# Sparse attention: the causal mask added to the scores in PSUM by VectorE, in one instruction with the row maximum

## The chip, the cores and the metric

The kernel runs on one core of a Trainium2 chip. The metric is the device time of one execution in microseconds (us). A core has five engines that take their instructions in a fixed order each, and wait for each other by semaphores: TensorE (PE in the profile; PEld is its weight load), VectorE (DVE), ScalarE (ACT), GpSimd (POOL) and SyncE (SP), which here issues the loads. TensorE writes its products to PSUM, eight banks of 128 partitions x 512 fp32; VectorE and ScalarE read and write both PSUM and SBUF.

## The reference

One decoder layer over 256 tokens of width 2048: gated linear attention and native sparse attention (NSA) beside each other, one output projection, then a SwiGLU FFN. The change lies in two of NSA's three branches, the selected blocks and the sliding window:

```
qh = rms_norm(heads(q, NSA_HEADS), q_g)          # 8 heads in 2 key/value groups
ss = einsum(qb, ks) * scale                      # selected blocks
ps = softmax(where(kpos <= t, ss, NEG))
o_sel = einsum(ps, vs)
sw = einsum(qb, kwb) * scale                     # sliding window
pw = softmax(where((wpos >= 0) & (dist >= 0) & (dist < WINDOW), sw, NEG))
o_win = einsum(pw, vwb)
```

With 256 tokens there are 4 blocks of 64 and all of them are selected (up to 16 may be), and the window of 512 covers the sequence. So both branches are plain causal attention, each with its own keys and values.

## The kernel before

Tokens are worked on in two tiles of 128 (t = 0, 1). The large products (L297 in `chunk`, L1178 in `gate_up`) are done in fp32 halves: a ScalarE copy makes the high part "hi" of a weight (L144), VectorE subtracts it to make the low part "lo" (L145, function `split`), and TensorE sums x_hi w_hi + x_hi w_lo + x_lo w_hi. One row of L145 makes the low part of two blocks of 128 weight rows, which then serve 12 matmuls.

The program is written as generators. `drive` runs a main one (a projection) and, for so many of its matmuls, one step of a side task: `gla_mix`, then `nsa_mix`. A scheduler then fixes each engine's order, so main and side matmuls alternate on TensorE. NSA runs beside the last piece of the query projection and beside `w_out_half(0)`, the first half of the output projection. It has four tiles of work, key/value group kv = 0, 1 by token tile t = 0, 1. For each of them `nsa_scores` works on four heads j, both branches b in one bank (view `sv`, 128 queries x 2 branches x ns keys, ns = 128 or 256):

- three matmuls (L902) make the scores in fp32 halves;
- a fourth product (L904) adds the mask to the last 128 keys of both branches: the stationary matrix is a bf16 identity `identb`, the moving one `cneg`, 0 or -1e30, in bf16 and twice beside each other;
- a short product (L905) makes the scores against the 15 compressed keys, into another bank;
- VectorE takes the maximum of each branch over its ns keys (L908) and scales it (L909);
- ScalarE takes the exponential with that bias and the row sum (L911), out of PSUM.

Then come the softmax of the compressed branch (L914 to L928) and the scaling of the probabilities (L934, eight rows a tile). `nsa_out` transposes the probabilities on TensorE (L215), evicts them in two parts by ScalarE (L665) and VectorE (L666), and multiplies them with the values (L976; L971 for the compressed branch, evicted by L959 and L960). Others that share VectorE in this stretch: L1014, which evicts a finished piece of `w_out_half`, L1110, sums of weight rows for the FFN, and L867 to L874, norms of the second query group.

The constants are made early in `constants()`: GpSimd writes the mask in fp32 to a scratch tile, VectorE casts it and the identity to bf16 (L436, L437).

Of the kernel before, what the change touches and what calls it, by code (L numbers as in the profile page):

```python
# [8 lines left out]
F32 = mybir.dt.float32  # L9
F32R = mybir.dt.float32r  # L10
BF16 = mybir.dt.bfloat16
AF = mybir.ActivationFunctionType
ALU = mybir.AluOpType
AX = mybir.AxisListType

P = 128
# [8 lines left out]
NEG = -1e30  # L25
# [12 lines left out]
def kernel(  # L38
# [4 lines left out]
    nc = tc.nc  # L43
    act, mm = nc.scalar.activation, nc.tensor.matmul
# [8 lines left out]
    cp = tc.alloc_tile_pool(name="cp", bufs=1)  # L53
# [5 lines left out]
    def slot(pool, tag, bufs, align=None):  # L59
        def f(shape, dt=F32):  # L60
            n_tiles[0] += 1
            return pool.tile([P] + list(shape), dt, tag=tag, bufs=bufs, name=f"{tag}_{n_tiles[0]}", align_bytes=align)
        return f
# [3 lines left out]
    g4, g2, g1, small = slot(gp, "g4", 24, LINE), slot(s2p, "g2", 13), slot(s1p, "g1", 7), slot(s1p, "sm", 12)  # L67

    def bank():
        n_tiles[0] += 1  # L70
        return pp.tile([P, 512], F32, tag="bank", name=f"bank_{n_tiles[0]}")
# [136 lines left out]
    ident = kp.tile([P, P], F32, name="ident")  # L208
# [199 lines left out]


    lmask = cp.tile([P, len(MASKED) + 2, P], F32, name="lmask")  # L410
    cneg = cp.tile([P, 2, P], BF16, name="cneg")
    identb = cp.tile([P, P], BF16, name="identb")
    mneg = cp.tile([P, NT, NCMP], F32, name="mneg")
    mone = cp.tile([P, NT, NCMP], F32, name="mone")

    def affine(ap, pattern, base, cm, fill=0.0):
        nc.gpsimd.affine_select(
            out=ap, in_=ap, pattern=pattern, compare_op=ALU.is_ge, fill=fill, base=base, channel_multiplier=cm)

    def constants():  # L420

        nc.gpsimd.memset(lmask, 1.0)
        affine(lmask[:, M_UP, :], [[1, P]], -1, -1)
        affine(lmask[:, M_LOW, :], [[-1, P]], -1, 1)
        for li, l in enumerate(MASKED):

            nb = P // (2 * l)
            v = lmask[:, li, :].rearrange("p (b h i) -> p b h i", h=2, i=l)
            for half, row0 in ((1, 0), (0, l)):
                affine(v[:, :, half, :], [[-2 * l, nb], [0, l]], -row0, 1)  # L430
                affine(v[:, :, half, :], [[2 * l, nb], [0, l]], row0 + l - 1, -1)

        cnegf = g1([2, P])
        nc.gpsimd.memset(cnegf, 0.0)
        affine(cnegf, [[0, 2], [-1, P]], 0, 1, NEG)
        nc.vector.tensor_copy(cneg, cnegf)  # L436
        nc.vector.tensor_copy(identb, ident)  # L437

        nc.gpsimd.memset(mneg, 0.0)
        affine(mneg, [[P, NT], [-16, NCMP]], -31, 1, NEG)  # L440
        nc.gpsimd.memset(mone, 1.0)
        affine(mone, [[P, NT], [-16, NCMP]], -31, 1, 0.0)
# [329 lines left out]
    def thrice(a):  # L772

        return a.unsqueeze(2).to_broadcast([P, a.shape[1], 3, NCMP])

    def groups(a):
        return a[:, :, :3 * G3].rearrange("p h (g n) -> p h g n", n=G3)[:, :, :, :NCMP]
# [110 lines left out]
    def nsa_scores(kv, t, res):  # L888
        ns, tb = (t + 1) * P, slice(t * P, (t + 1) * P)
        scv = sc[kv][:, t, :]  # L890
        qf, qh, ql = (a[:, :, tb] for a in nq[kv])
        kh, kl = (st[name][:, :, kv, :ns] for name in ("kh", "kl"))
        gv = st["gate"][:, t, 12 * kv:12 * kv + 12].rearrange("p (h b) -> p b h", b=3)
        pr = [g4([2, 2, ns]) for _ in range(2)] if t else [g4([4, 2, ns])]
        pr = [pr[j // 2][:, j % 2] if t else pr[0][:, j] for j in range(4)]
        mxs, nb, sums = small([4, 2]), small([4, 2]), small([4, 2])
        pc_ = bank()
        for j in range(4):
            p = bank()
            sv = p[:, :2 * ns].rearrange("p (b s) -> p b s", b=2)  # L900
            for i, (a, b) in enumerate(((qh, kh), (qh, kl), (ql, kh))):
                mm(sv, a[:, j], b, start=(i == 0), stop=False, skip_group_check=True)  # L902
                yield
            mm(sv[:, :, t * P:], identb, cneg, start=False, stop=True, skip_group_check=True)  # L904
            mm(pc_[:, j * NCMP:(j + 1) * NCMP], qf[:, j], kcm[:, kv * NCMP:(kv + 1) * NCMP],  # L905
               start=True, stop=True)
            yield
            nc.vector.tensor_reduce(mxs[:, j, :], sv, AX.X, ALU.max)  # L908
            TS(nb[:, j, :], mxs[:, j, :], scv[:, j:j + 1], -1.0, ALU.mult, ALU.mult)  # L909
            for b in range(2):  # L910
                act(pr[j][:, b, :], sv[:, b, :], AF.Exp, bias=nb[:, j, b:b + 1], scale=scv[:, j:j + 1],  # L911
                    accum_out=sums[:, j, b:b + 1])

        c = small([4, NCMP])  # L914
        TT(c, pc_[:, :4 * NCMP].rearrange("p (h n) -> p h n", h=4), scv.unsqueeze(2).to_broadcast([P, 4, NCMP]), ALU.mult)
        TT(c, c, mneg[:, t, :].unsqueeze(1).to_broadcast([P, 4, NCMP]), ALU.add)
        mx = small([4])
        nc.vector.tensor_reduce(mx, c, AX.X, ALU.max)
        TT(c, c, mx.unsqueeze(2).to_broadcast([P, 4, NCMP]), ALU.subtract)
        act(c, c, AF.Exp)  # L920
        sm = small([4])
        nc.vector.tensor_reduce(sm, c, AX.X, ALU.add)
        nc.vector.reciprocal(sm, sm)
        TT(sm, sm, gv[:, 0, :], ALU.mult)
        TT(c, c, mone[:, t, :].unsqueeze(1).to_broadcast([P, 4, NCMP]), ALU.mult)
        c3 = g2([4, P])
        nc.gpsimd.memset(c3, 0.0)
        TT(groups(c3), thrice(c), sm.unsqueeze(2).unsqueeze(3).to_broadcast([P, 4, 3, NCMP]), ALU.mult)  # L928
        rs = small([4, 2])
        nc.vector.reciprocal(rs, sums)  # L930
        TT(rs, rs, gv[:, 1:3, :].rearrange("p b h -> p h b"), ALU.mult)
        for j in range(4):
            for b in range(2):
                TS(pr[j][:, b, :], pr[j][:, b, :], rs[:, j, b:b + 1], None, ALU.mult)  # L934
        res.update(pr=pr, c=c3)
# [44 lines left out]
    def nsa_mix():  # L980
        tiles = [(kv, t) for kv in range(2) for t in range(NT)]
        res = {u: {} for u in tiles}

        def ready(u):
            while u[0] not in nq or not all(("key", br, t) in done for br in range(2) for t in range(NT)):
                yield

        for i, u in enumerate(tiles):
            yield from ready(u)
            yield from nsa_scores(*u, res[u])  # L990
            if i:
                yield from nsa_out(*tiles[i - 1], res[tiles[i - 1]])
        for _ in range(2):
            yield
        yield from nsa_out(*tiles[-1], res[tiles[-1]])
# [388 lines left out]

    drive([proj(C_LR, ev_go(0), ((0, 256), (256, 272)), first_chunk)], 2)
    constants()
    background += [sum_rows(f, pair) for f in sorted(SUMS) for pair in SUMS[f]]
    rate[0] = 12
# [56 lines left out]
```

## Time and profile before

| what | value |
|---|---|
| median of 3 runs | 1099.42 us (1099.35 to 1099.77) |
| the profiled execution, its own time | 1099.59 us |
| its span, first to last instruction | 1097.4 us |
| instructions in the trace | 14686 |
| first and last start of L902 | 286.0 and 338.6 us |
| data moved | 271.21 MB, mean 247 GB/s |

The profiled execution is 0.17 us above the median, and 2.2 us of it lie outside its span. The page gives each engine's busy share in 40 slices of 27.4 us each, as tenths:

```profile
PE   9999999999999999999999999999999999999998
DVE  6778879987799988997999999999999999999997
ACT  7755557555675587666585866768585867777785
PEclk9999999999999999999999999999999999999999
```

NSA lies in slices 11 to 14 from the left. TensorE is full everywhere, and its granted clock (PEclk) is full too. TensorE's starts are the reliable part of its rows: the ends are modelled and overlap, so the distance from one start to the next tells what a matmul takes on the path.

### The profile page before, as it was taken

The page shows a single profiled execution, that of the slowest core. Times are in us where ns is not written, and L with a number is a line of the kernel's source. Part 1 is how long each engine was busy: PE and PEld are TensorE (multiplying, and loading weights), DVE is VectorE, ACT ScalarE, POOL GpSimd, SP SyncE. Part 2 cuts the span into 40 slices and gives each one's busy share as a digit, 9 for nine tenths or more (in the row PEclk, how much of TensorE's full clock was granted, in tenths as well). Part 3 has the DMA queues.
Part 4 walks back from the last instruction along what each step waited for, and adds up shares of the span by engine and source line. Part 5 has one row for each costly group of instructions (what it writes and reads, how often), then busy time and mean ns, then how long its engine had stood idle before and what let it go on. Part 6 is the DMA issues. An engine that isn't in the chain of part 4 may idle for free.

```text
span 1097.4 us, 14686 instructions
## 1 busy us (share of the span) xinstructions
PE 1092.1 (100%) x5290; PEld 899.2 (82%) x5290; DVE 996.6 (91%) x1291; ACT 745.6 (68%) x1016; POOL 81.1 (7%) x150
## 2 busy tenths in 40 slices
PE   9999999999999999999999999999999999999998
PEld 8888888987777887888888888888888888888887
DVE  6778879987799988997999999999999999999997
ACT  7755557555675587666585866768585867777785
POOL 4100001032101100100000000000000000000000
PEclk9999999999999999999999999999999999999999
DMA  7999978468886956685576657576565768677663
GB/s 280 355 373 351 376 247 297 165 232 288 305 288 255 322 183 231 226 324 176 183 233 217 212 196 253 173 259 209 203 232 204 256 216 294 203 264 236 224 230 115
DMA packets 128884, 271.21 MB, mean 247 GB/s; under 512 B 7126, under 2 KB 9210, under 8 KB 128812
## 3 DMA queue, kind: packets, MB, share of 16 engines
q1 hardware_dynamic: 115532, 223.68, 59.4%
q0 software_dynamic: 12672, 46.14, 11.5%
q8 instruction: 41, 0.67, 0.2%
q10 hardware_dynamic: 608, 0.47, 0.1%
q14 instruction: 31, 0.25, 0.1%
HBM read 247.19 MB, written 23.07 MB: 246 GB/s over the span
## 4 chain that ended last, share of the span: by engine, by line
PE 94%; DVE 2%; issue 1%; ACT 1%; DMA 1%; SPq 0%; POOL 0%; DVEq 0%; POOLq 0%
PE bank L297 46%; PE bank L1178 39%; PE bank L215 3%; PE bank L1319 2%; DMA g<-in_x_dram 1%; PE bank L976 1%; PE bank L902 1%; DVE lo L145 1%; PE bank L607 0%; PE bank L809 0%; ACT hi L144 0%; ACT g L568 0%; PE bank L905 0%; PE bank L904 0%; POOL sm L218 0%
## 5 line engine op out<-in xcount | busy, mean ns | idle before, releaser
L1178 PE MATMUL bank<-ftwo,g 128*128 128x512 f32 x1842 | 430.6, 393 | 0.2 <-ACT ftwo L665 0.2
L1178 PEld LDWEIGHTS bank<-ftwo,g 128*128 128x128 f32 x1842 | 341.2, 188 | 76.8 <-DVE ftwo L666 3.9
L297 PE MATMUL bank<-hi,g 128*128 128x512 f32 (+1 forms) x1088 | 322.1, 376 | 0.4 <-ACT hi L348 0.4
L666 DVE TENSOR_TENSOR ftwo<-fraw,ftwo 128x1536 fp32r<-128x1536 f32 (+1 forms) x130 | 256.5, 1974 | 7.4 <-ACT ftwo L665 6.7
L665 ACT ACTIVATE ftwo<-fraw 128x1536 fp32r<-128x1536 f32 (+1 forms) x130 | 216.0, 1663 | 27.2 <-DMA fraw<-in_w_up_dram 17.1
L297 PE MATMUL bank<-ftwo,g 128*128 128x512 f32 x960 | 220.6, 390 | 0.0
L297 PEld LDWEIGHTS bank<-hi,g 128*128 128x128 f32 x1088 | 191.5, 188 | 30.6 <-issue 1.0
L297 PEld LDWEIGHTS bank<-ftwo,g 128*128 128x128 f32 x960 | 179.6, 188 | 38.3 <-ACT bank L1290 0.3
L297 PE MATMUL bank<-lo,g 128*128 128x512 f32 (+3 forms) x544 | 193.1, 375 | 0.1
L144 ACT ACTIVATE hi<-raw 128x1024 fp32r<-128x1024 f32 (+3 forms) x124 | 130.7, 1058 | 90.4 <-PE bank L297 67.0
L145 DVE TENSOR_TENSOR lo<-raw,hi 128x1024 fp32r<-128x1024 f32 (+3 forms) x124 | 150.0, 1216 | 33.0 <-ACT hi L144 32.5
L665 ACT ACTIVATE ftwo<-g 128x1024 fp32r<-128x1024 f32 x76 | 80.4, 1057 | 74.9 <-DVE g L1209 54.6
L297 PEld LDWEIGHTS bank<-lo,g 128*128 128x128 f32 x544 | 98.2, 189 | 14.5 <-DVE lo L145 0.3
L666 DVE TENSOR_TENSOR ftwo<-g,ftwo 128x1024 fp32r<-128x1024 f32 x76 | 92.6, 1219 | 10.7 <-ACT ftwo L665 10.7
L666 DVE TENSOR_TENSOR ftwo<-fsum,ftwo 128x1024 fp32r<-128x1024 f32 x76 | 92.5, 1218 | 1.0 <-ACT ftwo L665 1.0
L665 ACT ACTIVATE ftwo<-fsum 128x1024 fp32r<-128x1024 f32 x76 | 79.5, 1048 | 5.9 <-DVE fsum L1211 4.6
L1302 ACT COPY g<-bank 128x512 f32<-128x512 f32 x80 | 45.9, 588 | 38.4 <-PE bank L297 36.8
L1209 DVE TENSOR_TENSOR g<-fraw 128x1024 f32<-128x1024 f32 x54 | 65.2, 1217 | 0.0
L1290 ACT COPY bank<-g 128x512 f32<-128x512 f32 x80 | 45.3, 594 | 14.5 <-DVE f L1239 7.9
L1167 POOL DMA_DIRECT2D g<-sums x20 | 10.6, 532 | 501.9 <-DVE ftwo L666 473.3
L665 ACT ACTIVATE g<-bank 128x512 fp32r<-128x512 f32 x46 | 26.9, 597 | 29.6 <-PE bank L215 21.1
L215 PE MATMUL bank<-ident,g 128*128 128x128 f32 (+3 forms) x232 | 43.1, 276 | 0.1
(251 smaller groups left out, 909.5 us busy)
## 6 DMA issues: line engine op xcount, KB each, us to landing
fraw<-in_w_gate_dram SPq DMA_DIRECT2D x86, 512.0 KB, 3.8
fraw<-in_w_down_dram SPq DMA_DIRECT2D x42, 1024.0 KB, 5.0
raw<-in_w_in_dram SPq DMA_DIRECT2D x36, 1024.0 KB, 6.0
fraw<-in_w_up_dram SPq DMA_DIRECT2D x66, 512.0 KB, 4.8
sums<-g POOLq DMA_DIRECT2D x40, 512.0 KB, 6.5
raw<-in_w_out_dram SPq DMA_DIRECT2D x16, 1024.0 KB, 6.7
g<-in_w_gate_dram SPq DMA_DIRECT2D x20, 512.0 KB, 8.2
g<-in_w_up_dram SPq DMA_DIRECT2D x20, 512.0 KB, 9.9
```

The costliest lines, as they stand in the source:

```text
L144: act(h[:, i:i + n], r[:, k + i:k + i + n], AF.Copy)
L145: last["d"] = TT(o[:, i:i + n], r[:, k + i:k + i + n], f32(h[:, i:i + n]), ALU.subtract)
L215: return nc.tensor.transpose(o, i, ident[:n, :n])
L297: last["mm"] = mm(bk[t], a[:, k, t * P:(t + 1) * P], ws[k][m][:, off:off + w], start=(first_ and k == 0 and i == 0), stop=(end and k == 3 ...
L665: act(hi, ps, AF.Copy)
L666: last["d"] = TT(lo, ps, f32(hi), ALU.subtract)
L902: mm(sv, a[:, j], b, start=(i == 0), stop=False, skip_group_check=True)
L1178: mm(banks[q], x, m, start=todo[q] == total[q], stop=todo[q] == 1)
L1209: TT(s1, r[:, 1:3], r[:, 3:4].to_broadcast([P, 2, 512]), ALU.add)
L1290: last["seed", n] = nc.scalar.copy(banks[qs[n][t]], h_sb[n][:, t, :])
L1302: nc.scalar.copy(h_sb[n][:, t, :], bs[t])
L1319: mm(bk, u, m, start=(first and i == 0), stop=(end and i == 2), skip_group_check=onto)
```

## The change

The mask becomes an fp32 tile of 128 x 128 in SBUF, made by GpSimd alone; the bf16 identity and the two casts go. The product of the identity (L904) goes. In its place VectorE runs, for each head and branch, one fused instruction over the 128 keys of the tile's own block: it adds the mask to the scores, writes the sums back to the bank and takes their maximum. For t = 0 the maximum starts from -1e30; for t = 1 it starts from the maximum over the 128 earlier keys, which a reduction over both branches takes first (`past`).

```
-    cneg = cp.tile([P, 2, P], BF16, name="cneg")
-    identb = cp.tile([P, P], BF16, name="identb")
+    cneg = cp.tile([P, P], F32, name="cneg")
...
-        cnegf = g1([2, P])
-        nc.gpsimd.memset(cnegf, 0.0)
-        affine(cnegf, [[0, 2], [-1, P]], 0, 1, NEG)
-        nc.vector.tensor_copy(cneg, cnegf)
-        nc.vector.tensor_copy(identb, ident)
+        nc.gpsimd.memset(cneg, 0.0)
+        affine(cneg, [[-1, P]], 0, 1, NEG)
...
+        past = small([4, 2]) if t else None
         pc_ = bank()
         for j in range(4):
             p = bank()
             sv = p[:, :2 * ns].rearrange("p (b s) -> p b s", b=2)
             for i, (a, b) in enumerate(((qh, kh), (qh, kl), (ql, kh))):
-                mm(sv, a[:, j], b, start=(i == 0), stop=False, skip_group_check=True)
-                yield
-            mm(sv[:, :, t * P:], identb, cneg, start=False, stop=True, skip_group_check=True)
+                mm(sv, a[:, j], b, start=(i == 0), stop=(i == 2))
+                yield
             mm(pc_[:, j * NCMP:(j + 1) * NCMP], qf[:, j], kcm[:, kv * NCMP:(kv + 1) * NCMP],
                start=True, stop=True)
             yield
-            nc.vector.tensor_reduce(mxs[:, j, :], sv, AX.X, ALU.max)
+            if t:
+                nc.vector.tensor_reduce(past[:, j, :], sv[:, :, :P], AX.X, ALU.max)
+            for b in range(2):
+                own = sv[:, b, t * P:]
+                nc.vector.tensor_tensor_reduce(
+                    own, own, cneg, 1.0, past[:, j, b:b + 1] if t else NEG, ALU.add, ALU.max, mxs[:, j, b:b + 1])
             TS(nb[:, j, :], mxs[:, j, :], scv[:, j:j + 1], -1.0, ALU.mult, ALU.mult)
```

Lines shift: L902 of before is L899 in the changed kernel, L905 is L901, L909 is L910, and what follows is one line on; what stands in between `constants()` and `nsa_scores` is four lines back (L666 is L662). The new reduction is L905 there and the fused instruction L908.

The scheduler sets the order anew. TensorE, at the first head of the first tile, before (`bank_3001` holds its scores, `bank_3000` the compressed ones, the others are main work):

```order
L902 MATMUL bank_3001<-g_322_1985,g_496_2842 128x256
L297 MATMUL bank_2775<-lo_2957,g_58_362 128x512
L904 LDWEIGHTS identb
L904 MATMUL bank_3001<-cneg,identb 128x256
L905 MATMUL bank_3000<-kcm,g_494_2840 128x15
L297 MATMUL bank_2775<-hi_2956,g_59_363 128x512
```

and in the changed kernel:

```order
L899 MATMUL bank_2997<-g_321_1981,g_495_2838 128x256
L297 MATMUL bank_2771<-lo_2953,g_58_361 128x512
L901 MATMUL bank_2996<-kcm,g_493_2836 128x15
L297 MATMUL bank_2771<-hi_2952,g_59_362 128x512
L297 MATMUL bank_3033<-hi_3037,g_421_2504 128x512
```

The matmul of the mask is gone with its weight load; the short product follows the scores directly.

VectorE, before, at the third tile (kv = 1, t = 0), from the sixth to the ninth L145 after the first of `w_out_half(0)` (numbers 6 to 9; `bank_3385` and `bank_3411` are the scores of two heads, `sm` are small tiles):

```order
L145 TENSOR_TENSOR lo_3397<-raw_3394,hi_3396 128x2x512
L666 TENSOR_TENSOR g_579_3269<-bank_3270,g_578_3268 128x4x128
L145 TENSOR_TENSOR lo_3401<-raw_3394,hi_3400 128x2x512
L908 TENSOR_REDUCE sm_3347<-bank_3385 128x2
L908 TENSOR_REDUCE sm_3347<-bank_3411 128x2
L909 TENSOR_SCALAR sm_3348<-sm_3347,sc_3031 128x2 x2
L915 TENSOR_TENSOR sm_3426<-bank_3350,sc_3031 128x60
L145 TENSOR_TENSOR lo_3526<-raw_3523,hi_3525 128x2x512
L916 TENSOR_TENSOR sm_3426<-sm_3426,mneg 128x60
L145 TENSOR_TENSOR lo_3530<-raw_3523,hi_3529 128x2x512
```

In the changed kernel the same two heads behind number 7 (each fused instruction is a row ISA with its maximum fetched by a second row ISA of 128x1):

```order
L145 TENSOR_TENSOR lo_3401<-raw_3394,hi_3400 128x2x512
L908 ISA bank_3386,sm_3348<-bank_3386,cneg 128x128
L908 ISA sm_3348 128x1
L908 ISA bank_3412,sm_3348<-bank_3412,cneg 128x128
L908 ISA sm_3348 128x1
L908 ISA bank_3386,sm_3348<-bank_3386,cneg 128x128
L908 ISA sm_3348 128x1
L908 ISA bank_3412,sm_3348<-bank_3412,cneg 128x128
L908 ISA sm_3348 128x1
L910 TENSOR_SCALAR sm_3349<-sm_3348,sc_3026 128x2 x2
```

and, 17 rows on, what stands directly ahead of numbers 8 and 9:

```order
L929 TENSOR_TENSOR g_617_3439<-sm_3427,sm_3434 128x4x3x15
L935 TENSOR_SCALAR g_597_3347<-g_597_3347,sm_3442 128x128 x8
L662 TENSOR_TENSOR g_628_3484<-bank_3482,g_627_3483 128x512
L662 TENSOR_TENSOR g_631_3506<-bank_3504,g_630_3505 128x512
L1015 TENSOR_TENSOR g_596_3316<-bank_3304,g_596_3316 128x512
L1015 TENSOR_TENSOR g_596_3316<-bank_3305,g_596_3316 128x512
L145 TENSOR_TENSOR lo_3527<-raw_3524,hi_3526 128x2x512
L145 TENSOR_TENSOR lo_3531<-raw_3524,hi_3530 128x2x512
```

Two maxima became four fused instructions with four fetches, and numbers 8 and 9 moved behind the whole softmax of the tile, the scaling of its probabilities and the evictions.

## The prediction

> **What bounds the kernel now.** I read the page first, its busy shares and its chain that ended last.
>
> ```profile
> PE 1092.1 (100%) x5290; PEld 899.2 (82%) x5290; DVE 996.6 (91%) x1291; ACT 745.6 (68%) x1016; POOL 81.1 (7%) x150
> PE 94%; DVE 2%; issue 1%; ACT 1%; DMA 1%; SPq 0%; POOL 0%; DVEq 0%; POOLq 0%
> ```
>
> TensorE is busy for the whole span and 94% of the chain is its work: time that TensorE loses is time of the kernel. VectorE is the only other engine above 90%, so I next ask for the stretches around the edited lines, which run from 285 us (first L902) to about 360 us.
>
> ```profile
> core 0: us, PE busy (x) PEld busy (x) DVE busy (x) ACT busy (x) POOL busy (x), PEclk, DMA share, GB/s
> 285.00:360.00 75.00, 74.99 (x397) 59.53 (x396) 69.11 (x175) 47.96 (x125) 9.10 (x13) 1.00 0.77 280
> 360.00:420.00 60.00, 60.00 (x279) 48.60 (x278) 49.87 (x84) 45.33 (x74) 4.31 (x8) 1.00 0.66 230
> 420.00:1080.00 660.00, 659.75 (x2933) 539.02 (x2932) 639.67 (x599) 476.69 (x509) 20.37 (x39) 1.00 0.67 227
> ```
>
> VectorE is busy 69.1 of the 75 us in which the change sits; its cover is thin there. Whether it is thin enough shows only in the order of two engines: VectorE's rows L145 make the low part ("lo") of the weights that TensorE's main loop (L297) reads a little later. I number them from the first of `w_out_half(0)` as 0, and call them splits; split 2 starts at 285.38 us, 6 at 316.35 and 14 at 356.43.
>
> ```profile
> 285.38 1.22 DVE L145 TENSOR_TENSOR lo<-raw,hi 128x1024 fp32r<-128x1024 f32 x1
> 316.35 1.22 DVE L145 TENSOR_TENSOR lo<-raw,hi 128x1024 fp32r<-128x1024 f32 x1
> 317.93 0.47 PE L297 MATMUL bank<-lo,g 128*128 128x512 f32 x1
> 356.43 1.21 DVE L145 TENSOR_TENSOR lo<-raw,hi 128x1024 fp32r<-128x1024 f32 x1
> 358.01 0.40 PE L297 MATMUL bank<-lo,g 128*128 128x512 f32 x1
> ```
>
> Split 6 ends at 317.57 and the first matmul on its "lo" starts at 317.93; split 14 ends at 357.64 and its matmul starts at 358.01. At these two places VectorE is 0.4 us ahead of TensorE and no more. A longer VectorE row between splits 2 and 14 moves TensorE, unless VectorE gives up waiting time of its own. That waiting is in the waits view of the same stretch:
>
> ```profile
> DVE g L666 <- ACT g L665: 2.6, 4, 0.9
> DVE sc L874 <- POOL sc L218: 1.6, 1, 1.6
> DVE sm L922 <- ACT sm L920: 1.2, 1, 1.2
> ```
>
> It is 2.6 + 1.6 + 1.2 = 5.4 us. This is all the cover that the change has.
>
> **The change part by part.** (a) Sixteen products of the identity (L904) leave TensorE.
>
> ```profile
> L904 PE MATMUL bank<-cneg,identb 128*128 128x256 bf16 x16 | 4.5, 283 | 0.0
> 287.03 0.28 PE L904 MATMUL bank<-cneg,identb 128*128 128x256 bf16 x1
> 287.15 0.29 PE L905 MATMUL bank<-kcm,g 128*128 128x15 f32 x2
> ```
>
> The group's mean of 283 ns overlaps its neighbours; on the path one product costs the distance to the next start, 287.15 - 287.03 = 0.12 us. Sixteen are worth 16 x 0.115 = 1.8 us, if TensorE is what the stage waits for. Their weight loads lie under running matmuls and add nothing.
>
> (b) VectorE's sixteen row maxima (L908) shrink to eight over the earlier 128 keys only (for the second token tile), and 32 fused instructions of 128 columns come in, each followed in the order by a second row with a 128x1 output that fetches its maximum: 32 pairs. Durations overlap on VectorE too, so the prices are distances between starts; the forms view gives whole durations.
>
> ```profile
> 289.73 0.42 DVE L908 TENSOR_REDUCE sm<-bank 128x2 f32<-128x256 f32 x1
> 290.06 0.16 DVE L871 TENSOR_SCALAR sc<-sc 128x8 f32<-128x8 f32 x1
> 305.66 0.68 DVE L908 TENSOR_REDUCE sm<-bank 128x2 f32<-128x512 f32 x1
> 306.26 0.68 DVE L1110 TENSOR_TENSOR g<-g,g 128x512 f32<-128x512 f32 x1
> 383.96 0.28 DVE L1048 TENSOR_TENSOR g<-g 128x128 f32<-128x128 f32 x1
> 384.16 0.28 DVE L1047 TENSOR_TENSOR g<-g,g 128x128 f32<-128x128 f32 x1
> 296.82 0.16 DVE L924 TENSOR_TENSOR sm<-sm,gate 128x4 f32<-128x4 f32 x1
> 296.90 0.16 DVE L931 TENSOR_TENSOR sm<-sm,gate 128x8 f32<-128x8 f32 x1
> L612 DVE TENSOR_TENSOR g<-bank,ident 128x128 f32<-128x128 f32 x4 | 1.1, 286 | 0.0
> L924 DVE TENSOR_TENSOR sm<-sm,gate 128x4 f32<-128x4 f32 x4 | 0.7, 163 | 0.0
> L270 DVE SCALAR_TENSOR_TENSOR g<-bank,cols,g 128x256 fp32r<-128x256 f32 x14 | 6.1, 479 | 4.2 <-ACT g L268 4.2
> ```
>
> A maximum over 256 columns takes 290.06 - 289.73 = 0.33 us, one over 512 takes 306.26 - 305.66 = 0.60. Removed: 8 x 0.33 + 8 x 0.60 = 7.4 us. The eight maxima over the earlier keys read 256 columns again: 8 x 0.33 = 2.6 us added. The trace of before has no fused pair on VectorE, so it is bounded. Below: an ordinary 128x128 instruction steps 384.16 - 383.96 = 0.20 us, and the shortest small one 296.90 - 296.82 = 0.08, together 0.28. Above: both at whole durations, 286 (L612, PSUM and SBUF in, as here) and 163 ns (L924), together 0.45. ScalarE has such a pair, its exponential with the row sum:
>
> ```profile
> 317.91 0.45 ACT L911 ACTIVATE g<-bank,sm,sc 128x128 f32<-128x128 f32 x1
> 318.25 0.20 ACT L911 ACTIVATION_READ_ACCUMULATOR g<-bank,sm,sc 128x1 f32 x1
> 318.35 0.46 ACT L911 ACTIVATE g<-bank,sm,sc 128x128 f32<-128x128 f32 x1
> ```
>
> There the fetch starts 0.34 us into a 0.45 us instruction and the next one 0.10 later: the fetch overlaps, which speaks for the low end. For the high end speaks that the two halves of one bank are ordered by a wait, so the second pair often starts only when the first fetch is done. What a waiting successor costs:
>
> ```profile
> 293.30 0.42 DVE L908 TENSOR_REDUCE sm<-bank 128x2 f32<-128x256 f32 x1
> 293.75 0.23 DVE L909 TENSOR_SCALAR sm<-sm,sc 128x2 f32<-128x2 f32 x1
> ```
>
> L909 needs the maximum ahead of it and starts 0.45 after it, not 0.33. With part of the pairs alternating between two banks and part in such a sequence I take the middle, 0.36. Added: 32 x 0.36 = 11.5 us.
>
> [...]
>
> (c) The order moves. One more eviction (L666, a 0.60 step like the 512-wide maximum) now stands ahead of split 14, and the rows printed above show splits 8 and 9 behind the whole softmax of a tile, where before they stood between its instructions. Split 14 comes 6.7 + 0.6 = **7.3 us** later if VectorE keeps all its waits.
>
> (d) Of the 5.4 us of waits I let half go, 2.7 us: split 4 now stands between L919 and L922 and hides the 1.2; two pairs stand in the 1.6 us wait for GpSimd's square root and hide 0.7; a late VectorE finds ScalarE's results of L665 ready more often, 0.8 of 2.6. All 5.4 kept or all 5.4 gone are the ends. The change adds waits of its own: each second pair waits for the first, and behind it on VectorE's queue stand the splits and L666, for which TensorE's L297 and L976 wait.
>
> (e) Two casts of constants go.
>
> ```profile
> 2.31 0.26 DVE L437 CAST identb<-ident 128x128 bf16<-128x128 f32 x1 [1.11 <-POOL ident masks.py:199]
> 4.44 0.17 DVE L225 COPY cols<-bank 128x16 f32<-128x16 f32 x1 [1.87 <-PE bank L215]
> 22.91 0.28 DVE L436 CAST cneg<-g 128x256 bf16<-128x256 f32 x1
> 24.16 0.88 DVE L270 SCALAR_TENSOR_TENSOR g<-bank,cols,g 128x256 fp32r<-128x256 f32 x2 [0.97 <-ACT g L268]
> ```
>
> Behind both VectorE was idle anyway (1.87 us until TensorE, 0.97 until ScalarE): nothing. If that cover were gone they would be worth 0.5 us. SyncE's order of loads is the same in both; GpSimd's mask constant is half as wide, early and off the path: nothing either way.
>
> **Sum.** Split 14: +7.3 - 2.7, less its 0.4 us of slack = +4.2 us. The 1.8 us of (a) fall away here, because TensorE waits at that place whatever it saved ahead of it. Behind split 14 TensorE has the same work, and it has no idle time to give back there (659.75 of 660 us busy from 420 to 1080). The profiled execution took 1099.59 us (span 1097.4 and 2.2 around it), 0.17 above the median of the runs: 1103.8 beside it, **1103.6 us** as a median. Ends: waits all gone and pairs at 0.28 (32 x 0.08 = 2.6 less): +4.2 - 2.7 - 2.6 = -1.1; waits all kept and pairs at 0.45 (2.9 more): +4.2 + 2.7 + 2.9 = +9.8.
>
> **Rivals.**
> - *The cover holds* (ends on the other side: not slower). VectorE's new work goes wholly into waits, and TensorE stays the bound; then L904's 1.8 us are the result: 1097.6 us. It decides by whether VectorE's net growth ahead of split 14 stays under 5.4 + 0.4 = 5.8 us. For it: the low pair price gives 7.3 - 2.6 = 4.7. Against it: all three waits would have to vanish at once, and ScalarE's and GpSimd's rows that cause them are still there.
> - *The fused instruction is dear.* Should it pass its 128 columns twice, it costs what 128 more columns cost, 479 - 286 = 0.19 us (L270 against L612): 32 x 0.19 = +6.2, so 1109.8 us. Nothing in the trace shows such an instruction, for or against.
> - *The clock falls.* TensorE's granted clock is 1.00 in every window above, and it never paused there. The forecast makes it pause, some 6 us in all (4.2 and the lost 1.8), at two or three splits. If a pause halved the clock for as long as that pause, a matmul of 512 columns would step 0.46 us instead of 0.23 (L904 steps 0.115 for 256 columns) for 6 us, and the kernel would end 3 us later still: 1106.6 us. [...]
> - That the change does not do what it says is ruled out by the order: no row of L904 is left on TensorE.
>
> **How the numbers follow.** Forecast 0.62, cover holds 0.22, dear pair 0.10, clock 0.06. What a measurement here can tell from no change is about 0.2%, 2.2 us. The forecast's own bounds, -1.1 to +9.8, put about a seventh of its 0.62 under +2.2; "cover holds" lies within 0.2% but for a fifth of it, which is faster. So slower 0.53 + 0.16 = 0.69, same 0.09 + 0.17 = 0.26, faster 0.05. The range takes in both bounds of the unknown costs, from 1098.5 to 1109.4; what is left out is the full gain of "cover holds" and the top of the dear pair.
>
> **What would show it.** Right: L904 gone; some 32 rows of 0.2 to 0.3 us with a fetch behind each on VectorE; VectorE at 9.8 or more of every 10 us from 300 to 357; gaps of TensorE ahead of the first matmul on the "lo" of splits 6, 8 and 14; the stretch from 285 us to the first L1178 some 4 us longer and the rest unchanged. Wrong: TensorE's starts as dense as before (cover holds), pairs over 0.45 us (dear), or PEclk under 1.00 (clock). A loss outside 285 to 410 us would contradict all of it.

## The result and the profile after

The changed kernel takes **1105.5 us** (median of five runs, 1105.1 to 1106.8), the kernel before beside it 1099.77 (1099.35 to 1100.23): a ratio of 1.0055, 95% interval 1.0043 to 1.0066. It is slower by 5.7 us; 1103.6 was forecast, in a range of 1098.5 to 1109.4. The profiled execution is one of 1106.29 us, 0.8 above the median, so its losses add up to more than 5.7.

The page of the changed kernel, busy shares and chain:

```profile
PE 1094.0 (99%) x5274; PEld 900.2 (82%) x5274; DVE 1001.6 (91%) x1345; ACT 745.1 (67%) x1016; POOL 79.8 (7%) x150
PE 79%; DVE 10%; DMA 4%; issue 3%; ACT 3%; SPq 0%; POOL 0%; DVEq 0%; ACTq 0%; POOLq 0%
```

TensorE's share of the chain fell from 94% to 79%, and VectorE's rose from 2% to 10%: the chain now runs through VectorE where TensorE waits for it. How long TensorE waits itself, the windows of the prediction show for the changed kernel:

```profile
core 0: us, PE busy (x) PEld busy (x) DVE busy (x) ACT busy (x) POOL busy (x), PEclk, DMA share, GB/s
285.00:360.00 75.00, 72.24 (x369) 58.76 (x367) 70.21 (x228) 47.17 (x124) 8.02 (x13) 0.98 0.69 242
360.00:420.00 60.00, 58.41 (x268) 46.53 (x267) 51.41 (x82) 41.38 (x69) 2.84 (x5) 1.00 0.76 278
420.00:1080.00 660.00, 659.10 (x2925) 537.14 (x2924) 635.23 (x597) 474.02 (x505) 21.85 (x41) 1.00 0.67 226
```

TensorE has pauses of 2.8 us in the 75 us of NSA and 1.6 us in the 60 us behind it, and the granted clock is 0.98 in the first of these windows. Behind 420 us it is as busy as before but for 0.7 us. By the starts of its main matmuls the changed kernel is 5.1 us late at 420 us and 7.1 at the end: between 500 and 700 us the profiled execution loses another 1.0 and from 1020 us on 0.8, in the FFN, where no row was changed. `old_in_new_order`, a kernel of the experiments below with the same order, has no such steps there, so these losses are not put down to the change. TensorE's rows where the worst place lies, with the pause and its releaser in brackets:

```profile
317.54 0.66 PE L215 MATMUL bank<-ident,g 128*128 128x128 f32 x4 [1.06 <-DVE g L662]
318.93 0.80 PE L297 MATMUL bank<-lo,g 128*128 128x512 f32 x1 [0.74 <-DVE lo L145]
319.53 0.63 PE L297 MATMUL bank<-hi,g 128*128 128x512 f32 x1
319.95 0.63 PE L297 MATMUL bank<-lo,g 128*128 128x512 f32 x1
320.38 1.05 PE L297 MATMUL bank<-hi,g 128*128 128x512 f32 x2
...
361.82 0.50 PE L297 MATMUL bank<-lo,g 128*128 128x512 f32 x1 [0.31 <-DVE lo L145]
```

The second pause is one of those forecast, ahead of the first matmul on the "lo" of split 6; the last row is that of split 14, 3.8 us later than before (358.01). Behind split 6 the starts are 0.42 and 0.43 us apart, where a matmul of this form steps 0.23 in the kernel before (318.25 to 318.48): TensorE runs at half clock, 0.50 granted from 318.43 to 321.84 us. Windows of 2 us show how long:

```profile
316.00:318.00 2.00, 0.94 (x8) 0.69 (x6) 1.99 (x11) 0.60 (x1) 0.00 (x0) 1.00 1.05 409
318.00:320.00 2.00, 1.26 (x5) 0.87 (x4) 2.00 (x3) 1.77 (x7) 0.00 (x0) 0.61 1.04 411
320.00:322.00 2.00, 2.00 (x7) 1.52 (x6) 2.00 (x14) 1.45 (x8) 0.00 (x0) 0.54 1.04 411
322.00:324.00 2.00, 2.00 (x13) 1.68 (x12) 2.00 (x7) 2.00 (x8) 0.36 (x1) 1.00 1.05 391
```

Now VectorE at the same place, two heads of the third tile behind splits 6 and 7:

```profile
317.66 2.36 DVE L145 TENSOR_TENSOR lo<-raw,hi 128x1024 fp32r<-128x1024 f32 x2
319.93 0.29 DVE L908 CUSTOM_DVE_ANT_0 bank<-bank,cneg 128x128 f32<-128x128 f32 x1
320.14 0.14 DVE L908 DVE_READ_ACCUMULATOR2_ANT sm<- 128x1 f32 x1
320.14 0.33 DVE L908 CUSTOM_DVE_ANT_0 bank<-bank,cneg 128x128 f32<-128x128 f32 x1
320.39 0.14 DVE L908 DVE_READ_ACCUMULATOR2_ANT sm<- 128x1 f32 x1
320.39 0.33 DVE L908 CUSTOM_DVE_ANT_0 bank<-bank,cneg 128x128 f32<-128x128 f32 x1
```

Two things are to be seen. Split 6 starts at 317.66, 1.3 us later than before (316.35). And a pair is **cheap**: the next fused instruction starts together with the fetch, 0.21 to 0.25 us behind its forerunner. The pairs of the second token tile, whose maximum starts from `past`, step 0.27. Here the scheduler has woven the heads: the first halves of two heads, then the second halves, so that a row seldom waits for the one just ahead of it. Summed from start to start, without waits for other engines, the rows L905 and L908 of all sixteen heads take 11.1 us of VectorE, against 7.7 us of the old L908: a growth of 3.4 us where the prediction took 6.7. That is less than the 5.8 us under which the cover should have held, and yet the kernel is slower by more than forecast. So VectorE's added work can't be the whole reason.

The traces allow one more reading: how much later the main matmul (L297) of the same number starts than in the kernel before. Counted from the first of `w_out_half(0)`, matmul 72 is the first of the piece of splits 6 and 7. Its row in the kernel before, and below it the one in the changed kernel:

```profile
316.76 0.48 PE L297 MATMUL bank<-hi,g 128*128 128x512 f32 x1
314.34 0.71 PE L297 MATMUL bank<-hi,g 128*128 128x512 f32 x2
```

It starts 2.4 us **earlier**; two further on, at the first lo, the changed kernel is 1.0 us late (318.93 against 317.93). TensorE's new order postpones side work, the main loop runs ahead, and it wants split 6 earlier just when VectorE brings it later. When the postponed side work is done (near 340 us) 2.4 us are lost, at 361 us 3.5, and a second step of 1.6 us follows at 383 us:

```profile
384.22 0.33 PE L215 MATMUL bank<-ident,g 128*128 128x128 f32 x1 [1.00 <-ACT g L1075]
384.84 0.33 PE L215 MATMUL bank<-ident,g 128*128 128x128 f32 x1 [0.28 <-ACT g L1075]
```

Split 8 starts 11.3 us later than before (331.55 against 320.27) without a pause of TensorE, since the side work was moved ahead of it there as well.

### The profile page after: what moved, and what is told of

It is laid out like the page before. It is cut to its first block, busy times and chain, and to the rows that moved or that the text cites. A ratio compares the mean times of both kernels' runs of the same rounds, so it can differ in the third digit from the quotient of the medians.

```text
span 1104.4 us, 14707 instructions
## 1 busy us (share of the span) xinstructions
PE 1094.0 (99%) x5274; PEld 900.2 (82%) x5274; DVE 1001.6 (91%) x1345; ACT 745.1 (67%) x1016; POOL 79.8 (7%) x150
## 4 chain that ended last, share of the span: by engine, by line
PE 79%; DVE 10%; DMA 4%; issue 3%; ACT 3%; SPq 0%; POOL 0%; DVEq 0%; ACTq 0%; POOLq 0%
PE bank L297 39%; PE bank L1179 34%; DVE ftwo L662 3%; PE bank L215 2%; PE bank L1320 2%; DMA fraw<-in_w_up_dram 2%; DVE lo L145 2%; DMA raw<-in_w_out_dram 1%; DMA g<-in_x_dram 1%; DVE g L1210 1%; ACT ftwo L661 1%; DVE g L662 1%; ACT hi L144 1%; DVE g L1111 1%; DVE fsum L1212 0%
## 5 line engine op out<-in xcount | busy, mean ns | idle before, releaser
L297 PE MATMUL bank<-hi,g 128*128 128x512 f32 (+1 forms) x1088 | 319.7, 376 | 0.4 <-ACT hi L348 0.4
L662 DVE TENSOR_TENSOR ftwo<-fraw,ftwo 128x1536 fp32r<-128x1536 f32 (+1 forms) x130 | 256.7, 1976 | 8.1 <-ACT ftwo L661 7.0
L661 ACT ACTIVATE ftwo<-fraw 128x1536 fp32r<-128x1536 f32 (+1 forms) x130 | 216.0, 1663 | 28.7 <-DMA fraw<-in_w_up_dram 19.1
L297 PE MATMUL bank<-ftwo,g 128*128 128x512 f32 x960 | 220.7, 390 | 0.0
L297 PEld LDWEIGHTS bank<-hi,g 128*128 128x128 f32 x1088 | 191.9, 189 | 30.8 <-issue 1.0
L297 PEld LDWEIGHTS bank<-ftwo,g 128*128 128x128 f32 x960 | 179.6, 188 | 38.4 <-ACT bank L1291 0.3
L297 PE MATMUL bank<-lo,g 128*128 128x512 f32 (+3 forms) x544 | 194.0, 377 | 1.1 <-DVE lo L145 1.0
L145 DVE TENSOR_TENSOR lo<-raw,hi 128x1024 fp32r<-128x1024 f32 (+3 forms) x124 | 150.0, 1218 | 33.8 <-ACT hi L144 33.2
L661 ACT ACTIVATE ftwo<-g 128x1024 fp32r<-128x1024 f32 x76 | 80.4, 1057 | 74.9 <-DVE g L1210 51.6
L297 PEld LDWEIGHTS bank<-lo,g 128*128 128x128 f32 x544 | 98.6, 189 | 16.6 <-DVE lo L145 2.0
L662 DVE TENSOR_TENSOR ftwo<-g,ftwo 128x1024 fp32r<-128x1024 f32 x76 | 92.7, 1220 | 9.9 <-ACT ftwo L661 9.9
L662 DVE TENSOR_TENSOR ftwo<-fsum,ftwo 128x1024 fp32r<-128x1024 f32 x76 | 92.6, 1219 | 0.5 <-ACT ftwo L661 0.5
L661 ACT ACTIVATE ftwo<-fsum 128x1024 fp32r<-128x1024 f32 x76 | 79.6, 1048 | 7.0 <-DVE fsum L1212 5.6
L661 ACT ACTIVATE g<-bank 128x512 fp32r<-128x512 f32 x46 | 27.2, 600 | 34.5 <-PE bank L215 22.2
L215 PE MATMUL bank<-ident,g 128*128 128x128 f32 (+3 forms) x232 | 42.3, 276 | 2.9 <-ACT g L1075 1.3
```

Of the source, the lines that this page charges most:

```text
L145: last["d"] = TT(o[:, i:i + n], r[:, k + i:k + i + n], f32(h[:, i:i + n]), ALU.subtract)
L215: return nc.tensor.transpose(o, i, ident[:n, :n])
L297: last["mm"] = mm(bk[t], a[:, k, t * P:(t + 1) * P], ws[k][m][:, off:off + w], start=(first_ and k == 0 and i == 0), stop=(end and k == 3 ...
L661: act(hi, ps, AF.Copy)
L662: last["d"] = TT(lo, ps, f32(hi), ALU.subtract)
```

## The experiments

Theory O: the scheduler's new **order** makes the loss. Theory W: VectorE's new **work** makes it, in any order. All times are medians beside runs of the kernel before on the same chip (1099.3 to 1099.8 us each time). In brackets stands the ratio to the kernel before with its 95% interval; it can differ a little from the quotient of the two medians.

### One part at a time

`nomask`: the kernel before without the product (and so without the mask in these branches).

```
-                mm(sv, a[:, j], b, start=(i == 0), stop=False, skip_group_check=True)
+                mm(sv, a[:, j], b, start=(i == 0), stop=(i == 2))
                 yield
-            mm(sv[:, :, t * P:], identb, cneg, start=False, stop=True, skip_group_check=True)
```

> The kernel before without the product of the identity, so the mask of the two branches is left out; the maxima stay as they were. This is TensorE's part alone. Both theories give the same here if the order stays: sixteen products of 0.115 us go, about -1.8 us against the kernel before (1097.9 us), unless VectorE holds the stage already, in which case nothing is gained there (1099.8 us). The clock stays at 1.00.

`both`: the product stays, and VectorE's fused instruction runs with a tile of zeros.

```
+            if t:
+                nc.vector.tensor_reduce(past[:, j, :], sv[:, :, :P], AX.X, ALU.max)
+            for b in range(2):
+                own = sv[:, b, t * P:]
+                nc.vector.tensor_tensor_reduce(
+                    own, own, zero, 1.0, past[:, j, b:b + 1] if t else NEG, ALU.add, ALU.max, mxs[:, j, b:b + 1])
-            nc.vector.tensor_reduce(mxs[:, j, :], sv, AX.X, ALU.max)
```

> The product of the identity stays and the fused instruction runs as well, with a tile of zeros in place of the mask. This is VectorE's part, with the order that it brings, alone. Theory 'VectorE sets the stage' (its order and waits decide when the splits come): TensorE's products are hidden in its pauses, so the time is that of the changed kernel, 1105 to 1106 us, not 1.8 us more. Rival 'the costs add': the changed kernel's time and 16 x 0.115 us, 1107.3 us. If the loss came from the missing product and not from VectorE, the time would be about that of the kernel before, 1100 us.

`nomask` took 1103.35 us (1.0031, 1.0020 to 1.0042), `both` 1106.87 (1.0063, 1.0051 to 1.0075). The first is a miss for every theory: work was taken away, and the kernel became slower. Its profiled execution took 1100.96 us, the lowest of eight; where the others lose more is in no trace. In this one `nomask` gains 0.7 us from 285 to 361 us, as it should; then it loses 2.3 us at one place, the transposes of the normed residual:

```profile
380.59 0.33 PE L215 MATMUL bank<-ident,g 128*128 128x128 f32 x1 [1.67 <-ACT g L1073]
381.21 0.33 PE L215 MATMUL bank<-ident,g 128*128 128x128 f32 x1 [0.29 <-ACT g L1073]
```

ScalarE comes late there because its queue stood still, by its waits view:

```profile
ACT hi L144 <- DMA raw<-in_w_out_dram: 3.0, 1, 3.0
```

The changed kernel's second step, at 383 us, stands at the same transposes, behind a wait of ScalarE for a load of `w_out`, 3.0 us as well. A few rows in another order upset a place 40 us behind. `both` shows that the fused instructions with the order that comes with them lose at least as much as the change does; whether the product costs something on top (0.9 us by the ratios) can't be told, since the intervals overlap and its order is a third one.

### The splits earlier

`hoist_after` and `hoist_before`: each piece's fetch and split is written one piece ahead.

```
-                ws = split(fetch(w_out[0], 4 * i, 4, n * 512, 512), 4, 512)
+                ws = ahead.pop((n, c), None) or weights(n, c)
+                if half == 0 and (n, c) != (3, 1):
+                    ahead[n + c, 1 - c] = weights(n + c, 1 - c)
```

> The changed kernel with the fetch and the split of each piece of the output projection's first half written one piece ahead, so that the scheduler sets the splits earlier on VectorE. VectorE's work is the same. Theory 'order': the loss comes from splits 6 to 9 standing behind the softmax, scaling and evictions of a tile; with the splits ahead of these most of the 5.7 us goes, 1098 to 1101 us, and the granted clock stays at 1.00. Rival 'work': VectorE has too much to do in this stretch in any order, and the time stays within 1.5 us of the changed kernel's, 1104 to 1107 us.

> The kernel before with the same earlier fetch and split: the control. Both theories: TensorE loses next to nothing in the kernel before, so nothing is to be had; within 1 us of it, 1099 to 1101 us. If this kernel gains as much as the hoisted changed kernel does, the gain there would be of its own and say nothing on the order that the change brought.

1109.24 us (1.0083, 1.0070 to 1.0096) and 1102.39 (1.0026, 1.0017 to 1.0034): both slower, outside what either theory gave. With the splits in front TensorE waits for the softmax instead; three of its rows in `hoist_after`:

```profile
307.97 3.45 PE L215 MATMUL bank<-ident,g 128*128 128x128 f32 x15 [2.30 <-ACT g L912]
328.57 1.09 PE L215 MATMUL bank<-ident,g 128*128 128x128 f32 x8 [1.64 <-ACT g L912]
331.70 0.77 PE L977 MATMUL bank<-g,g 128*128 128x512 f32 x1 [2.04 <-ACT g L661]
```

So "late splits" was too narrow a theory: TensorE waits along two paths, the splits and the softmax chain (maxima on VectorE, exponentials L912 on ScalarE, transposes L215). That what is put ahead on one is taken from the other is argued: the hoist moved other rows as well.

### Work and order apart

The two can be parted cleanly. At the end of the program each instruction of an engine in this stretch is tied behind the one that shall stand ahead of it (an edge that orders, without a wait), so that the scheduler must keep a given order. Every work can then be run in every order.

```
+    for engine, base, runs in orders:
+        own = [i for i in traced if i.engine == engine]
+        row = [own[base + a + k] for a, n in runs for k in range(n)]
+        for a, b in zip(row, row[1:]):
+            tc.add_manual_dep(b, a.name, mybir.DependencyInfo(
+                mybir.DependencyClass.NoSync, mybir.DependencyReason.DATA), reason="order")
```

> The changed kernel, with the scheduler held to the order of the kernel before on TensorE, VectorE and ScalarE: in the place of each old maximum stand the fused pairs of its head. The work is that of the changed kernel to the instruction. Theory 'order': the loss comes from the order alone. VectorE's real growth, 32 pairs of 0.25 us and eight maxima of 0.33 for sixteen of 0.33 and 0.60, is 8.0 + 2.6 - 7.4 = 3.2 us, which its 5.4 us of waits in that stretch cover, so TensorE keeps the 1.8 us of the sixteen products: 1097.8 us, at most 1099.5, clock 1.00. Rival 'work': the fused instructions are too much for VectorE in any order: 1103 to 1106 us.

> The kernel before, with its product of the identity and its plain maxima, held to the order of the changed kernel on TensorE, VectorE and ScalarE. Theory 'order': it is as slow as the changed kernel though nothing of its work is changed, 1104 to 1107 us, with TensorE's pauses at the same places (ahead of the first matmul on the lo part of splits 6 and 8, and in the transposes near 383 us) and a clock of 0.998. Rival 'work': without the new VectorE work it is as fast as the kernel before, 1099 to 1101 us.

> The kernel before without the product of the identity (the mask of the two branches is left out), held to the order of the kernel before. Without that hold it took 1100.96 to 1106.06 us. Theory 'order': the sixteen products give their 1.8 us, 1097.8 us, and the spread of some 5 us between executions goes. Rival: something in the missing products themselves costs time (the clock, or bank timing): 1101 to 1104 us as without the hold.

> The product of the identity stays and the fused instruction adds a tile of zeros, held to the order of the kernel before: VectorE's part alone, without its order. Without that hold it took 1106.87 us. Theory 'order': 3.2 us more on VectorE vanish in its waits, 1099.6 to 1100.6 us. Rival 'work': 1103 to 1107 us. A result between, 1101 to 1103, would put part of the loss on VectorE's work.

| work | in the scheduler's order for it | in the order of the kernel before | in the order of the changed kernel |
|---|---|---|---|
| of the kernel before | 1099.6 | the same | **1106.61** (1.0054, 1.0042 to 1.0067) |
| of the changed kernel | 1105.5 (1.0055) | **1103.84** (1.0037, 1.0023 to 1.0050) | the same |
| `nomask` | 1103.35 | **1098.48** (0.9990, 0.9982 to 0.9999) | not run |
| `both` | 1106.87 | **1103.73** (1.0036, 1.0023 to 1.0048) | not run |

The old work in the new order is as slow as the changed kernel: theory O holds, and the new order alone costs all of the loss. By the medians it is 7.0 us, by the ratio 5.9; the five executions took 1103.9 to 1107.0 us, and the profiled one is the lowest. The kernel before held to its own order was not run; 1098.48 us for `nomask` speaks against the hold itself being dear. TensorE's pauses in the new order stand at the same two rows as in the changed kernel:

```profile
318.36 0.66 PE L215 MATMUL bank<-ident,g 128*128 128x128 f32 x4 [0.93 <-DVE g L666]
319.75 0.50 PE L297 MATMUL bank<-lo,g 128*128 128x512 f32 x1 [0.73 <-DVE lo L145]
```

But the new work in the old order is slow too, by 4.3 us: theory W holds as well, and the two losses don't add. VectorE's rows in `new_in_old_order`, one head of the second tile and the start of the next row:

```profile
297.58 0.42 DVE L905 TENSOR_REDUCE sm<-bank 128x2 f32<-128x256 f32 x1
298.04 0.36 DVE L908 CUSTOM_DVE_ANT_0 bank<-bank,cneg,sm 128x128 f32<-128x128 f32 x1
298.31 0.14 DVE L908 DVE_READ_ACCUMULATOR2_ANT sm<- 128x1 f32 x1
298.49 0.36 DVE L908 CUSTOM_DVE_ANT_0 bank<-bank,cneg,sm 128x128 f32<-128x128 f32 x1
298.77 0.14 DVE L908 DVE_READ_ACCUMULATOR2_ANT sm<- 128x1 f32 x1
298.77 0.34 DVE L929 TENSOR_TENSOR g<-sm,sm 128x180 f32<-128x180 f32 x1
```

Here the maximum ahead costs 0.46 us instead of 0.33, since the fused instruction waits for it, and the first pair 0.45 instead of 0.27, since the second waits for its fetch (0.18 us, from 298.31 to 298.49). A head takes 1.19 us where the old maximum took 0.60. All sixteen take 14.6 us, a growth of 6.9. TensorE's pauses in this kernel are mainly ahead of the transposes and value products of the softmax chain, and ScalarE's exponentials in it wait 9.5 us for VectorE's scaled maxima (3.6 us in the kernel before). TensorE's rows, and that line of the waits view:

```profile
302.11 0.44 PE L215 MATMUL bank<-ident,g 128*128 128x128 f32 x2 [1.29 <-ACT g L912]
308.20 0.42 PE L215 MATMUL bank<-ident,g 128*79 128x128 f32 x2 [0.79 <-issue]
310.30 0.47 PE L977 MATMUL bank<-g,g 128*128 128x512 f32 x1 [0.49 <-DVE sm L916]
320.73 0.50 PE L297 MATMUL bank<-lo,g 128*128 128x512 f32 x1 [0.72 <-DVE lo L145]
347.31 0.47 PE L977 MATMUL bank<-g,g 128*128 128x512 f32 x1 [1.11 <-DVE sm L916]
ACT g L912 <- DVE sm L910: 9.5, 6, 2.0
```

Without the fused instructions the old order gives the product's gain, 1.1 us (`nomask_in_old_order`; 0.1 to 2.0 by its interval). With them it makes no difference whether the product is there (1103.84 against 1103.73): TensorE waits for VectorE anyway.

### Cheap pairs in the old order

So the old order has dear pairs and early splits, the new one cheap pairs and late splits. `woven` takes both good halves: the old order, with the rows of a head parted by one or two neighbours. VectorE's order, f0 and f1 being the two fused instructions of head j and R its reduction over the earlier keys:

```
-  R(5) f0(5) f1(5) R(6) f0(6) f1(6) L910 L910 L145 L145
+  R(5) R(6) f0(5) f0(6) f1(5) f1(6) L910 L910 L145 L145
...
-  R(4) f0(4) f1(4) L929 L935 x8
+  R(4) L929 f0(4) L935 f1(4) L935 x7
```

> The changed kernel in the order of the kernel before on TensorE and ScalarE; on VectorE too, except that the fused instructions of a head are parted by one or two rows that stood next to them (another head's, an L935, an L1111, an L867), since in the old order each second half of a pair waited for the first one's fetch and each pair for the maximum ahead of it: the sixteen heads' rows cost 14.6 us from start to start there, 11.1 in the changed kernel's own order and 7.7 in the kernel before. The splits stay where the kernel before has them. Theory 'price of the dependent pair' (in the old order it is the waits inside the pairs that exhaust VectorE's cover, in the new order the place of the splits): VectorE's growth falls from 6.9 to about 3.5 us, under its 5.4 us of waits, and TensorE keeps most of its 1.8 us: 1098 to 1100.5 us. Rival 'any growth on VectorE shows, since TensorE also waits for the softmax chain that runs through it': half of the growth stays, 1101 to 1103 us.

1099.92 us, 1.0005 of the kernel before (0.9996 to 1.0014). Nearly all of the changed kernel's loss is gone with no change in what is computed. The rows of the two heads of the diff's first lines:

```profile
300.93 0.74 DVE L905 TENSOR_REDUCE sm<-bank 128x2 f32<-128x256 f32 x2
301.60 0.35 DVE L908 CUSTOM_DVE_ANT_0 bank<-bank,cneg,sm 128x128 f32<-128x128 f32 x1
301.86 0.14 DVE L908 DVE_READ_ACCUMULATOR2_ANT sm<- 128x1 f32 x1
301.86 0.35 DVE L908 CUSTOM_DVE_ANT_0 bank<-bank,cneg,sm 128x128 f32<-128x128 f32 x1
302.13 0.14 DVE L908 DVE_READ_ACCUMULATOR2_ANT sm<- 128x1 f32 x1
```

0.26 and 0.27 us a pair; the sixteen heads take 11.0 us, a growth of 3.3. The three forced orders give the price of VectorE's growth: none (`nomask_in_old_order`) 1098.48, 3.3 us 1099.92, 6.9 us 1103.84. The first 3.3 us cost 1.4, the next 3.6 cost 3.9 (1.6 and 3.5 by the ratios). The profiled execution of `woven` took 1102.36 us, the highest of eleven; it was 1.7 us late already at 285 us, ahead of NSA.

### Which engine's order

Three more, each with its edit in the list of orders alone: only VectorE's woven order held; only TensorE's and ScalarE's old order held; and `woven` with one row moved, the scaled maximum (L910) of head 4 directly behind its pairs instead of six L935 later.

> The changed kernel with only VectorE's order held, to that of the woven kernel (1099.92 us); TensorE's and ScalarE's orders are left to the scheduler. Theory 'splits': VectorE's order, with the splits where the kernel before has them, is what matters, and TensorE's side work may stand a little otherwise: 1099.5 to 1101.5 us. Rival 'TensorE's side work': the clumps that the scheduler makes of score matmuls, transposes and value products wait for VectorE and ScalarE whatever VectorE's order is: 1103 to 1106 us, with waits of L215 and L977 and none of L297 for lo.

> The changed kernel with only TensorE's and ScalarE's order held, to that of the kernel before; VectorE's is left to the scheduler, which then sets four splits and several evictions at other places than either kernel has them. Theory 'splits': VectorE's order decides, so holding TensorE's alone brings at most half of the 5.7 us back: 1102.5 to 1106 us. Rival 'TensorE's side work': holding it brings nearly all back, 1099 to 1101 us.

> The woven kernel with one row moved: the scaled maximum (L910) of the first head of the second tile stands six rows of L935 earlier, directly behind its maximum, so that ScalarE's exponential of that head can start some 1.2 us earlier. If the loss that is left near 300 to 310 us (1.0 to 1.6 us against the kernel before's place) comes from ScalarE's wait for that row, 1098.6 to 1099.5 us, which would be the fastest of the kernels that do the whole work; if it comes from VectorE's growth itself, no change, 1099.5 to 1100.3 us.

1102.03 us (1.0025, 1.0014 to 1.0036), 1102.11 (1.0024, 1.0013 to 1.0035) and 1099.99 (1.0008, 0.9999 to 1.0017). Either engine's order brings back some 3.4 of the 5.7 us and neither brings back all: of each pair of theories the truth lies between. Held alone, VectorE's order leaves TensorE waiting for a split (first row below, `woven_vector_alone`); TensorE's order alone leaves it waiting for the softmax and its evictions (second and third, `tensor_alone`):

```profile
319.10 0.50 PE L297 MATMUL bank<-lo,g 128*128 128x512 f32 x1 [1.08 <-DVE lo L145]
...
302.04 0.44 PE L215 MATMUL bank<-ident,g 128*128 128x128 f32 x2 [1.39 <-ACT g L912]
310.06 0.50 PE L977 MATMUL bank<-g,g 128*128 128x512 f32 x1 [1.65 <-ACT g L661]
```

The earlier L910 changes nothing: what `woven` still loses near 300 to 310 us (1.3 us in both traces) isn't ScalarE's wait for that row. The traces name an eviction of VectorE, in `woven` and `woven_bias_early`:

```profile
310.33 0.50 PE L297 MATMUL bank<-hi,g 128*128 128x512 f32 x1 [0.67 <-DVE g L662]
308.66 0.50 PE L297 MATMUL bank<-hi,g 128*128 128x512 f32 x1 [0.68 <-DVE g L662]
```

No kernel that does the whole work was faster than the kernel before.

## Why the prediction was right in sign and range, and short in size

- **What bounds the kernel** held. TensorE was full and VectorE 0.4 us ahead at splits 6 and 14; the loss lies where VectorE is late. That the splits are the only path was wrong: the softmax chain (L215 behind L912, L977 behind L661) is as thin, and `hoist_after` and `tensor_alone` show it.
- **(a)** The products' 1.8 us fall away where TensorE waits: shown in the old order, by 1103.84 with them gone and 1103.73 with them kept. With VectorE's old work they are worth 1.1 us (`nomask_in_old_order`). What they are worth in the changed kernel's own order was not measured.
- **(b)** The pair price of 0.36 us was mis-sized for the changed kernel, where a pair steps 0.21 to 0.28 (one 0.32), at or below the lower bound of 0.28, since the row behind the fetch starts together with it (320.14 and 320.39 us in the rows above). For the old order it was nearly right, 0.34 on average: the first pair of a head costs 0.45 us for the second token tile and some 0.4 for the first, its second pair 0.28 and 0.22. That the whole growth is 6.9 us against 6.7 in the sum is partly luck: the eight maxima cost 0.45 each there, not 0.33. The same pair cost 0.45 us where the next one waited for its fetch and 0.21 to 0.28 where it did not, so the price went by the neighbours, and the prediction named the cause (a wait between the two halves of one bank) without seeing that the new order avoids it.
- **(c)** The step that failed. The moved splits were seen in the order, and only one L666 (0.6 us) was put into the sum for the whole move. The order's price is 5.9 us by the ratio of `old_in_new_order` (0.0054 of 1099.6), with no new work at all. The sum needed the distance between two moves: TensorE's main loop came 2.4 us earlier to the piece of split 6 and VectorE's split 1.3 us later.
- **(d)** "Half of the waits" was too much. In the old order growths of 3.3 and 6.9 us cost 1.4 and 5.4 us, so 1.9 and 1.5 us were hidden; the prediction let 2.7 + 0.4 go. In the changed kernel VectorE's gaps between splits 2 and 14 shrank by 1.1 us (5.9 to 4.8, all gaps counted), and the wait for GpSimd's square root, which was to hide 0.7, stayed at 1.5.
- **The sum.** In the changed kernel split 14 starts 4.1 us later (360.55 against 356.43) where the sum had 4.6, and its first matmul 3.8 us later where it had 4.2. That is near, but with other parts, so it is luck in part: VectorE's rows between splits 2 and 14 grew by 5.3 us (some 3.5 by the maxima and fused rows, 0.7 by the one L666 more, the rest in rows beside them, of which L934 0.5), and 1.1 us of its gaps went. What the sum is short by lies behind split 14, where it let TensorE lose nothing more: the step of 1.6 us at 383 us. The +4.3 us of `new_in_old_order` equal the forecast too, but on another path: of its pauses shown above, 3.7 us lie ahead of transposes (L215) and value products (L977) and 0.7 at split 6.
- **Rivals.** "Cover holds" is almost what `woven` is, 1099.92 us: with the splits in place more than half of 3.3 us of growth vanishes. Its criterion (growth under 5.8 us) was met by the changed kernel and did not decide. "Dear pair" fell: no pair of the changed kernel steps more than 0.32 us. "The clock falls" was right as a part: half clock for 3.4 us, in which TensorE, at a step of 0.42 instead of 0.23 us, does some 1.6 us less. How much of that reaches the end is not shown, since TensorE waits for VectorE again at split 14.
- **The places.** The pauses ahead of "lo" at splits 6 and 14 were there, that at split 8 was not. VectorE was busy 9.98 and 9.90 us of each 10 up to 320 us, and 9.35 to 9.53 from there to 350, less than the 9.8 expected. The loss at 383 us lies inside the 285 to 410 us that were named, but by a path (a late load that holds up ScalarE) that the prediction did not have.

What stays open: why the scheduler set these rows otherwise; its own estimates are in no trace. How far the step at 383 us is the order's doing was not tried by itself, and why the load ahead of it comes late was not followed up. Between 361 and 410 us five of the six kernels with TensorE's order held to the old one lose under 0.3 us (`woven` 0.7), six of the other seven 0.9 to 3.2.

## What to carry to other kernels

Where two engines run in fixed orders with tenths of a microsecond between them (0.4 us at splits 6 and 14 here), an edit that lets a scheduler set the order anew is first a change of order, and taking work away can make such a kernel slower, as `nomask` was by 0.31%; run new work in the old order, and old work in the new, before judging either. Of short dependent instructions take the price from their neighbours: with a row of another head between them the pairs cost 0.26 and 0.27 us in `woven`, where the first pair of a head had cost 0.45. And a group that is cheaper on its own engine (11.1 us in the new order, 14.6 in the old) may push aside what another engine waits for (split 6, 1.3 us later).

## What the runs showed of the hardware

- **The granted clock fell to half for 3.4 us.** In the changed kernel's trace it is 0.50 for 3.413 us, from 318.43 us on, and 1.00 for 314.03 us ahead of that and 781.65 us behind it, 92 and 229 times as long. In one window of 10 us each it is 0.83 in `both` (320 to 330), `tensor_alone` (310 to 320) and `hoist_after` (330 to 340), which is what 3.4 us at half make. In the 3.41 us ahead of the half clock TensorE paused for 1.30 us in the changed kernel, by its modelled busy time; the pause of 1.06 us shown above lies in them, and that of 0.74 reaches from them into the half clock. Pauses as long had no such sequel elsewhere: in `new_in_old_order` TensorE paused for 2.3 us between 300 and 310 us, 1.29 of them in one piece, and in the changed kernel for 1.3 us between 380 and 390 (1.00 and 0.28), both at a granted clock of 1.00. What decides is not shown.
- **The spread follows the clock in part.** `old_in_new_order` took 1103.9 and 1104.9 us in the executions with a mean clock of 0.999 or more, and 1106.6, 1106.8 and 1107.0 in those with 0.998; `nomask` 1101.0 to 1102.2 and 1103.0 to 1106.1. That a half-clock stretch makes the whole difference is not shown: `both` took 1106.2 to 1107.0 us at 1.000 and 1106.2 and 1107.6 at 0.998, `tensor_alone` 1101.1 to 1103.1 at 1.000 and 1102.3 at 0.998.
- **The fetch of the maximum** takes no start distance of its own (0.00 us to the next row, as at 320.14 us in the changed kernel) unless the next row waits for it (0.17 to 0.18 us, as from 298.31 to 298.49 in `new_in_old_order`). From a fused instruction to its fetch the step in the changed kernel is 0.26 to 0.28 us where the start value comes from a small tile, and 0.21 to 0.25 (one 0.32) where it is the constant.
